# Column-quarter w_mod sums, host-made layouts, two-bank accounting and smaller first loads in a two-block transformer kernel

## The chip, the core and the metric

The program runs on one core of one Trainium2 chip. The metric is the device time of one execution in microseconds (us), taken as the median of three executions.

## What is computed

The reference takes 256 rows of 2048 features through two blocks, all in float32, batch 1.

Block one: `x + 0.5 * swiglu(rms_norm(x))` with inner width 5632; a mixer (`rms_norm(x) @ w_in`, grouped attention with rotary positions beside differential attention, `@ w_out`, residual); a second such feed-forward; a closing `rms_norm`.

Block two: two layers over x and, in layer 0, over a second stream, the context (256 rows of 2048). Each layer first makes modulation vectors, `silu(c) @ w_mod + b_mod` and `silu(c_ctx) @ w_mod + b_mod` (2048 x 6144 weights, one input row each), split into shift, scale and gate. The streams are normalised, scaled and shifted (`h = rms_norm(x) * (1 + scale) + shift`), projected by `w_in` (2048 x 6656), taken through pooling, neighbourhood attention (local window plus context keys, 16 heads of 64) and a depthwise convolution, gated, and projected by `w_out`. A last `rms_norm` closes it.

## The kernel before, in words

Every large product runs on TensorE (PE). Weights come in pieces of 512 x 512 (1 MB, `raw0` to `raw2`, three buffers), are split in halves of 256 rows by ScalarE (ACT) into `hi` (rounded to fp32r) and by VectorE (DVE) into `lo` (the rest), four halves in flight. Activations, transposed, lie in SBUF as operands `g` in the same two parts. For each contraction tile of 128 and each of two row tiles PE does three fp32r matmuls of 512 columns (`xh*hi`, `xh*lo`, `xl*hi`), so a piece is 24 matmuls and a half 12.

The program is written out instruction by instruction (`tc.manual_schedule`). `Net.run` walks the list of weight halves and emits their matmuls; after each group of three, `pump` lets "lanes" (Python generators: attention items, transposes, norms, convolution) emit their next steps. A planner keeps estimated clocks for PE, DVE and ACT (`tP`, `tD`, `tA`) and estimated end times of the last write (`W`) and read (`R`) of each tile. A lane that yields "pe" is resumed when `tP` has passed the lane's time `me.t` by 200 ns; after a load it waits 8000 ns (`DMA_LAT`, L32). So PE's order is fixed when the program is made, and where an estimate is early PE stands still on the chip.

PSUM: four banks belong to two jobs in turn, three are "side" banks for the lanes, one (`pv`) is for attention outputs. `get` (L312) hands out slots of a pool; for side banks it sets `me.t` to the time at which the last reader of the first slot handed out is done (L325). Attention items of block two (`item_x`, `item_c`) take two side banks at once, put the scores of one head of 64 in each, and read each by a maximum and an exponential.

At the start `consts` loads the identity and the gains of the first norm, `warm` (L715) issues WARM = 4 matmuls on zeros, and `first_loads` (L792) loads x by 512 columns between the first pieces. `next_norm` and `gain_op` transpose x on PE (four 128 x 128 per side bank, L252) and write the operand `f1h`. `setup_lane` (L727) starts at 25 us: silu of c, the other gains, the convolution taps and the lambda of block one; gains and taps are loaded as rows and transposed on PE.

`wmod_step` multiplies w_mod pieces of 128 x 1024 by the entries of the two input rows and adds them on DVE, so that a job (12 in all, 6 for each layer) ends with two accumulators of 128 x 1024, whose sums over the 128 partitions are wanted. `wmod_sum` (L919) splits each in hi and lo and multiplies it with a column of ones (`sel`): per accumulator two groups of 512 columns, in each a pair of fp32r matmuls, one row read out, one store.

`mod_op` (L1377) prepares the operand of a layer: load rows, scale by the row's 1/rms, transpose on PE, scale and shift, split. For the context of layer 0 it is `c0h`.

SP issues nearly all loads and stores, in program order. `mm`, `act`, `tt`, `stt` record each operation, so matmuls stand at L224, transposes at L252, ACT at L157, DVE at L167 and L176.

Of the kernel before, what the change touches and what calls it, by code (L numbers as in the profile page):

```python
# [16 lines left out]
D = 2048  # L17
# [14 lines left out]
DMA_LAT = 8000.0  # L32
WARM = 4
SLACK = [2500.0, 2000.0, 1500.0, 0.0, 0.0]
# [73 lines left out]
class Net:  # L108
# [338 lines left out]
    def run(self, seq):  # L447
# [14 lines left out]
        def fetch():  # L462
            while at["fetch"] < len(pieces):
# [23 lines left out]
                self.dmaT = max(self.dmaT, self.R.get(n, 0.0), self.tP - 8000) + t  # L487
                self.W[n] = max(self.dmaT, self.R.get(n, 0.0) + t + 2000)
# [57 lines left out]
        for h, (job, i, s) in enumerate(main):  # L546
# [22 lines left out]
            for z, kt in enumerate(kts):  # L569
# [5 lines left out]
                for t in range(2):  # L575
                    self.slot += 1
                    m = slice(t * 128, t * 128 + 128)
                    self.mm(job.ps[t], xh[:, m], hi[:, z, :], st, False, ready)
                    self.mm(job.ps[t], xh[:, m], lo[:, z, :], False, False, ready)
                    self.mm(job.ps[t], xl[:, m], hi[:, z, :], False, sp, ready)  # L580
# [100 lines left out]
    def consts(self):  # L681
# [11 lines left out]
        self.csil = self.cp.tile([128, 2, 16], F32, name="csil")  # L693
        self.sel = self.cp.tile([128, 2], F32R, name="sel")
        self.wleft = [6, 6]
# [5 lines left out]
        self.lam = self.keep(1)  # L701
        self.f1rows = self.cp.tile([16, 128], F32, name="f1rows")
# [3 lines left out]
    def consts_lane(self):  # L706
        b, = yield from self.get("side")
        ps = self.bank(b)
        self.tr(ps[:, :16], self.f1rows, self.ident[:16, :16])
        self.copy(self.fv[:, 0:16], ps[:, :16])  # L710
        self.rel(b)
        self.flags.add("f1gain")
        yield

# [12 lines left out]
    def setup_lane(self):  # L727
        a = self.a

        yield from self.after(25)  # L730
        s, s2 = yield from self.get("T2", 2)
# [3 lines left out]
        self.dma(c[:, 1, :], a["c_ctx_2"].rearrange("(p k) -> p k", p=128))  # L735
        self.dma(self.blob[:, 128:576], a["k_blob"][:, 128:576])
        yield "dma"
# [3 lines left out]
        self.ts(self.csil, c, 0.5)  # L741
        one = self.sb(s2, [128, 2])
        self.nc.vector.memset(one, 1.0)
        self.copy(self.sel, one)
        self.rel(s, s2)
        self.flags.add("cs")

        s, = yield from self.get("T2")
        fr = self.sb(s, [128, 128])
        for nm, key in (("mix_norm", "mix"), ("ffn2_norm", "f2"), ("norm_g_2", "ng0"), ("conv_dw_b_2", "cdb"),  # L750
                        ("conv_ln_g_2", "lng"), ("conv_ln_b_2", "lnb"), ("b_subln", "bsub"), ("pool_scale_2", "psc")):
            src = a[nm].rearrange("o (r c) -> (o r) c", c=128)
            self.dma(fr[FV[key] - 16:FV[key] - 16 + src.shape[0], :], src)
        yield "dma"
        b, = yield from self.get("side")
        ps = self.bank(b)
        n = NFV - 16
        self.tr(ps[:, :n], fr[:n, :], self.ident[:n, :n])
        yield "evA"
        self.copy(self.fv[:, 16:NFV], ps[:, :n])  # L760
        self.rel(b, s)
        yield "D"
# [3 lines left out]
        s, = yield from self.get("T2")  # L766
        w = self.sb(s, [128, 512])
        self.dma(w[:62, :], a["conv_dw_2"].rearrange("l k c -> (l k) c"))
        yield "dma"
        b, = yield from self.get("side")  # L770
        ps = self.bank(b)
        for i in range(4):
            self.tr(ps[:, i * 62:i * 62 + 62], w[:62, i * 128:i * 128 + 128], self.ident[:62, :62])
        yield "ev"
        self.copy(self.cdw.rearrange("p c k -> p (c k)"), ps[:, :248])
        self.rel(b, s)

# [14 lines left out]
    def first_loads(self, n):  # L792

        cs = slice(n * 512, n * 512 + 512)
        self.nc.sync.dma_start(out=self.x[:, :, cs], in_=self.xin[:, :, cs])
        self.dmaT += 1475
        for t in range(2):
            self.W[self.key(self.x[:, t, cs])] = self.dmaT

        def later(n=n, t=self.dmaT):  # L800
            yield from self.until("f1gain")
            while self.tP < t:
                yield lambda: self.tP >= t
            yield from self.next_norm("f1", n)

        self.spawn(later(), 0)

# [111 lines left out]
    def wmod_sum(self, job):  # L919

        l, c = job.wmod
        for r in range(2):
            hs, ls = yield from self.get("T4", 2)
            hi, lo = self.sb(hs, [128, 1024], F32R), self.sb(ls, [128, 1024], F32R)
            yield from self.lsplit(hi, lo, job.acc[r])
            self.rel(job.slots[r])
            for z in range(2):
                cs = slice(z * 512, z * 512 + 512)
                b, = yield from self.get("side")
                yield "pe"  # L930
                ps = self.bank(b)
                self.mm(ps[:2, :], self.sel, hi[:, cs], True, False)
                self.mm(ps[:2, :], self.sel, lo[:, cs], False, True)
                s, = yield from self.get("T2")
                yield "evA"
                row = self.sb(s, [128, 512])
                self.copy(row[:1, :], ps[:1, :])
                self.rel(b)
                yield "st"
                self.dma(self.modrows[l][r:r + 1, c * 1024 + z * 512:c * 1024 + z * 512 + 512], row[:1, :])  # L940
                self.rel(s)
            self.rel(hs, ls)
# [371 lines left out]
    def next_norm(self, f, n):  # L1314
# [3 lines left out]
        yield from self.gain_op(f + "h", n, self.x, f)  # L1318
        if f == "f1":
            self.cur.prio = 3  # L1320
            yield from self.after(22)
        for t in range(2):
            yield from self.sq_part(self.x[:, t, cs], ssp[:, 4 * t + n:4 * t + n + 1])
        self.vals[f + "_left"] -= 1
        if self.vals[f + "_left"] == 0:
# [51 lines left out]
    def mod_op(self, op, src, rstd, rflag, l, w):  # L1377
# [3 lines left out]
        for n in range(4):  # L1381
# [7 lines left out]
            for j in range(2):  # L1389
# [13 lines left out]
                yield  # L1403
            self.rel(*sl)

    def chunk_pieces(self, wt, col):
# [619 lines left out]
    def body(self, upto):  # L2026
# [9 lines left out]
        self.xin = a["x"][0].rearrange("(t p) d -> p t d", p=128)  # L2036
        self.dmaT = 3550.0
        self.vals = {}
# [23 lines left out]
        self.warm()  # L2062
        self.spawn(self.consts_lane(), 0)
        self.first_loads(0)
# [38 lines left out]


# [15 lines left out]
```

## Time and profile before

| What | Value |
|---|---|
| Median of 3 executions | 3276.68 us (3273.68 to 3277.45) |
| Profiled execution, its own time | 3275.49 us |
| Its span in the profile | 3273.7 us |
| PE busy | 3250.8 us, 99% |
| DVE busy | 2560.0 us, 78% |
| ACT busy | 1588.7 us, 49% |
| HBM read | 702.58 MB |

The page lists engines, the chain of work that ended last, and groups of instructions. A matmul on float32 tiles shows as two records, one on fp32r as one. "Busy" of PE counts a modelled end, so for prices the starts of the next instructions are used, not the durations. A wait is written "engine tile line <- what ended it".

### The profile page before, as it was taken

The page shows a single profiled execution, that of the slowest core. Times are in us where ns is not written, and L with a number is a line of the kernel's source. Part 1 is how long each engine was busy: PE and PEld are TensorE (multiplying, and loading weights), DVE is VectorE, ACT ScalarE, POOL GpSimd, SP SyncE. Part 2 cuts the span into 40 slices and gives each one's busy share as a digit, 9 for nine tenths or more (in the row PEclk, how much of TensorE's full clock was granted, in tenths as well). Part 3 has the DMA queues.
Part 4 walks back from the last instruction along what each step waited for, and adds up shares of the span by engine and source line. Part 5 has one row for each costly group of instructions (what it writes and reads, how often), then busy time and mean ns, then how long its engine had stood idle before and what let it go on. Part 6 is the DMA issues. An engine that isn't in the chain of part 4 may idle for free.

```text
span 3273.7 us, 40054 instructions
## 1 busy us (share of the span) xinstructions
PE 3250.8 (99%) x15284; PEld 2649.1 (81%) x15284; DVE 2560.0 (78%) x3418; ACT 1588.7 (49%) x2086; POOL 1.2 (0%) x11
## 2 busy tenths in 40 slices
PE   9999999999999999999999999999999999999998
PEld 7888888888888888888888877788877788887777
DVE  5998999866876689988888588666887676598766
ACT  5544444445555444444445554544454455445543
POOL 0000000000000000000000000000000000000000
PEclk9999999999999999999999999999999999999999
DMA  7877777755445677777776665477555576564555
GB/s 246 293 275 274 268 272 278 279 196 183 146 163 168 229 261 273 264 269 263 271 266 228 206 196 167 154 231 238 181 159 151 163 242 229 182 191 136 166 174 188
DMA packets 362581, 713.79 MB, mean 218 GB/s; under 512 B 40180, under 2 KB 43814, under 8 KB 362388
## 3 DMA queue, kind: packets, MB, share of 16 engines
q1 hardware_dynamic: 362388, 711.23, 65.2%
q8 instruction: 120, 1.97, 0.2%
q14 instruction: 73, 0.60, 0.0%
HBM read 702.58 MB, written 8.59 MB: 217 GB/s over the span
## 4 chain that ended last, share of the span: by engine, by line
PE 93%; DVE 3%; DMA 2%; issue 1%; ACT 0%; SPq 0%; ACTq 0%; DVEq 0%
PE mm L224 85%; PE side L252 4%; PE side L224 3%; DVE T L176 2%; DMA T<-in_na_rpb 1%; PE pv L224 1%; DVE lo L167 1%; DVE T L167 0%; DMA xs<-res 0%; ACT hi L157 0%; ACT T L157 0%; DMA res<-in_x 0%; SPq L258 0%; DVE sm L184 0%; DVE side L167 0%
## 5 line engine op out<-in xcount | busy, mean ns | idle before, releaser
L224 PE MATMUL mm<-hi,g 128*128 128x512 f32 x8576 | 2747.1, 394 | 0.7 <-ACT hi L157 0.7
L224 PEld LDWEIGHTS mm<-hi,g 128*128 128x128 f32 x8576 | 1612.6, 188 | 351.3 <-issue 17.9
L167 DVE TENSOR_TENSOR lo<-raw,hi 128x1024 fp32r<-128x1024 f32 (+1 forms) x1079 | 1312.1, 1221 | 480.1 <-ACT hi L157 477.6
L224 PE MATMUL mm<-lo,g 128*128 128x512 f32 x4288 | 1672.5, 390 | 0.4 <-DVE lo L167 0.4
L157 ACT ACTIVATE hi<-raw 128x1024 fp32r<-128x1024 f32 (+1 forms) x1079 | 1140.0, 1059 | 1096.0 <-PE mm L224 967.5
L224 PEld LDWEIGHTS mm<-lo,g 128*128 128x128 f32 x4288 | 807.4, 188 | 159.9 <-DVE lo L167 1.3
L176 DVE SCALAR_TENSOR_TENSOR T<-T,csil,T 128x1024 f32<-128x1024 f32 x360 | 445.2, 1278 | 0.0
L157 ACT ACTIVATE T<-side 128x512 f32<-128x512 f32 (+2 forms) x180 | 104.6, 584 | 183.2 <-PE side L252 130.4
L252 PEld LDWEIGHTS side<-blob,T 128*128 128x128 f32 (+1 forms) x1027 | 125.5, 140 | 37.3 <-issue 6.3
L252 PE MATMUL side<-blob,T 128*128 128x128 f32 (+1 forms) x1027 | 154.5, 274 | 0.1
L176 DVE SCALAR_TENSOR_TENSOR T<-Y,cdw,T 128x256 f32<-128x256 f32 x360 | 151.0, 478 | 0.0
L157 ACT ACTIVATE T<-side,sm 128x256 f32<-128x256 f32 (+1 forms) x131 | 74.9, 577 | 65.5 <-DVE sm L184 49.7
L157 ACT ACTIVATE T<-T 128x512 f32<-128x512 f32 (+5 forms) x91 | 65.6, 721 | 59.4 <-DVE T L167 47.2
L167 DVE TENSOR_TENSOR T<-T,T 128x512 f32<-128x512 f32 (+4 forms) x130 | 81.9, 651 | 7.3 <-ACT T L157 5.1
L224 PE MATMUL side<-T,T 128*128 128x256 f32 (+2 forms) x352 | 76.3, 377 | 7.6 <-ACT T L157 4.1
L184 DVE TENSOR_REDUCE sm<-side 128x1 f32<-128x512 f32 (+1 forms) x96 | 65.8, 690 | 11.3 <-PE side L224 8.8
L224 PEld LDWEIGHTS side<-T,T 128*128 128x128 f32 (+1 forms) x352 | 51.0, 188 | 25.8 <-issue 10.0
L157 ACT ACTIVATE g<-side 128x512 fp32r<-128x512 f32 (+1 forms) x58 | 32.9, 569 | 79.0 <-PE side L252 72.6
L176 DVE SCALAR_TENSOR_TENSOR res<-mm,res 128x512 f32<-128x512 f32 x96 | 61.6, 681 | 0.6 <-PE mm L224 0.6
L167 DVE TENSOR_TENSOR T<-T,blob 128x256 f32<-128x256 f32 (+2 forms) x80 | 39.4, 526 | 17.3 <-DMA T<-in_na_rpb 15.3
L157 ACT ACTIVATE T<-mm 128x512 f32<-128x512 f32 x66 | 38.7, 597 | 29.0 <-PE mm L224 25.6
L157 ACT ACTIVATE T<-mm,kp 128x512 f32<-128x512 f32 (+1 forms) x58 | 39.1, 682 | 26.3 <-PE mm L224 24.0
(99 smaller groups left out, 926.1 us busy)
## 6 DMA issues: line engine op xcount, KB each, us to landing
raw<-in_w_in SPq DMA_DIRECT2D x208, 1024.0 KB
raw<-in_ffn_w_gu SPq DMA_DIRECT2D x175, 1024.0 KB
T<-in_w_mod SPq DMA_DIRECT2D x192, 512.0 KB
raw<-in_ffn_w_down SPq DMA_DIRECT2D x88, 1024.0 KB
raw<-in_w_out SPq DMA_DIRECT2D x64, 1024.0 KB
T<-xs SPq DMA_DIRECT2D x32, 256.0 KB
T<-in_ctx SPq DMA_DIRECT2D x24, 256.0 KB
T<-in_na_rpb SPq DMA_DIRECT2D x64, 96.0 KB
```

Source lines behind the costliest of these rows:

```text
L157: self.nc.scalar.activation(out, in_, func, **kw)
L167: self.nc.vector.tensor_tensor(out=out, in0=in0, in1=in1, op=op)
L176: self.nc.vector.scalar_tensor_tensor(out=out, in0=in0, scalar=s, in1=in1, op0=op0, op1=op1)
L184: self.nc.vector.reduce_max(out=out, in_=in_, axis=AX.X, negate=True)
L224: self.nc.tensor.matmul(out, lhsT, rhs, start=start, stop=stop)
L252: self.nc.tensor.transpose(out, in_, self.ident if ident is None else ident)
```

## The change

Six things are done:

1. `wmod_sum` no longer splits. It multiplies the four accumulator halves as float32 with 32 columns of ones, each into 32 partitions of one side bank (column quarters 0, 32, 64, 96), reads the bank once and stores four rows.
2. `host_layouts` adds four inputs: x transposed in blocks, the context transposed, the gains as columns, the taps as columns. Block one's first operand comes from the transposed x (`first_op`), with no PE transposes. The rows of x are loaded later, with pieces 3 to 6, for the sums of squares (`first_sums`) and the residual. `setup_lane` starts at 45 us and has no transposes.
3. `ctx_op` takes the place of `mod_op` for `c0h`: it spreads the rows' 1/rms over all partitions by two float32 matmuls of ones with a diagonal, and multiplies the transposed context by it.
4. `get` sets `me.t` to the latest of all side banks handed out.
5. Loads at the start: x first, by half a block; piece 0 in three parts; the gains on ACT's queue; WARM = 6; the planner's first due times are altered.
6. In the first half the order is `xh*hi`, `xl*hi`, `xh*lo`.

```diff
-WARM = 4
+WARM = 6
...
         if pool == "side":
-            me.t = max(me.t, self.R.get(self.last.get(got[0]), 0.0))
+            me.t = max([me.t] + [self.R.get(self.last.get(g), 0.0) for g in got])
...
                 if p == 0:
-                    for z in range(2):
-                        self.nc.sync.dma_start(out=raws[p][:, 2 * z:2 * z + 2], in_=ap[:, 2 * z:2 * z + 2])
+                    for z in (slice(0, 1), slice(1, 2), slice(2, 4)):
+                        self.nc.sync.dma_start(out=raws[p][:, z], in_=ap[:, z])
...
-                if p < 3:
+                if p < 9:
                     self.first_loads(p + 1)
...
+                    three = [(xh, hi), (xh, lo), (xl, hi)]
+                    if h == 0:
+                        three = [three[0], three[2], three[1]]
...
-        nc.sync.dma_start(out=self.ident, in_=a["k_blob"][:, 0:128])
-        nc.sync.dma_start(out=self.f1rows, in_=a["ffn1_norm"].rearrange("o (r c) -> (o r) c", c=128))
+        nc.scalar.dma_start(out=self.fv, in_=a["h_fv"])
...
-        yield from self.after(25)
+        yield from self.after(45)
...
     def first_loads(self, n):
+        if n < 4:
+            if n == 0:
+                self.xT = [self.sb(self.pools["T4"].free.pop(0), [128, 4, 256]) for _ in range(4)]
+            for i, z in ((0, slice(0, 2)),) if n == 0 else ((0, slice(2, 4)), (1, slice(0, 4))) if n == 1 else ((n, slice(0, 4)),):
+                self.nc.sync.dma_start(out=self.xT[i][:, z], in_=self.a["h_x"][i][:, z])
+            gen = self.first_op
+        elif n < 8:
+            cs = slice((n - 4) * 512, (n - 4) * 512 + 512)
+            self.nc.sync.dma_start(out=self.x[:, :, cs], in_=self.xin[:, :, cs])
+            gen = self.first_sums
...
+    def first_op(self, n):
+        for zs in ((0,), (1,), (2, 3)) if n == 0 else ((0, 1), (2, 3)):
+            g = yield from self.gran("f1h", (4 * n) // 8)
+            part = [(4 * n + z, self.xT[n][:, z, :], self.fv[:, FV["f1"] + 4 * n + z:FV["f1"] + 4 * n + z + 1]) for z in zs]
+            for kt, src, f in part:
+                self.act(g[:, 0, kt % 8, :], src, AF.Copy, scale=f)
+            yield "D"
+            for kt, src, f in part:
+                self.stt(g[:, 1, kt % 8, :], src, f, g[:, 0, kt % 8, :].bitcast(F32), ALU.mult, ALU.subtract)
...
     def wmod_sum(self, job):
-        for r in range(2):
-            hs, ls = yield from self.get("T4", 2)
-            yield from self.lsplit(hi, lo, job.acc[r])
-            for z in range(2):
-                self.mm(ps[:2, :], self.sel, hi[:, cs], True, False)
-                self.mm(ps[:2, :], self.sel, lo[:, cs], False, True)
-                self.copy(row[:1, :], ps[:1, :])
+        for r in range(2):
+            for z in range(2):
+                q = 2 * r + z
+                self.mm(ps[32 * q:32 * q + 32, :], self.sel, job.acc[r][:, z * 512:z * 512 + 512], True, True)
+        self.copy(rows, ps)
+        for q in range(4):
+            self.dma(self.modrows[l][q // 2:q // 2 + 1, at:at + 512], rows[32 * q:32 * q + 1, :])
...
+    def ctx_op(self, op):
+        for t in range(2):
+            self.ts(dg[:, t, :], self.ident, rstd[:, t:t + 1])
+        for t in range(2):
+            self.mm(ps[:, t * 128:t * 128 + 128], self.ones, dg[:, t, :], True, True)
+        for z in range(2):
+            self.copy(R[:, z, :], ps[:, :256])
+        for n in range(4):
+            for j in range(2):
+                self.dma(v[j], self.a["h_ctx"][kt * 128:kt * 128 + 256].rearrange("(k p) t -> p k t", p=128))
+            for j in range(2):
+                self.tt(y, y, R, ALU.mult)
+                for z in range(2):
+                    self.affine(y[:, z, :], y[:, z, :], self.modA[0][:, 16 + kt + z:17 + kt + z], ...)
+                yield from self.lsplit(g[:, 0, k:k + 2, :], g[:, 1, k:k + 2, :], y)
...
-            self.spawn(self.mod_op("c0h", a["ctx_2"][0], self.vals["c0_rstd"], "c0_rstd", 0, 1), 1)
+            self.spawn(self.ctx_op("c0h"), 1)
...
+def host_layouts(a):
+    fv = np.concatenate([a[n].reshape(-1, 128).T for n in (
+    cdw = a["conv_dw_2"].reshape(62, 4, 128).transpose(2, 1, 0)
+    x = a["x"][0].T.reshape(4, 4, 128, T).transpose(0, 2, 1, 3)
+    return [("h_x", x), ("h_ctx", a["ctx_2"][0].T), ("h_fv", fv), ("h_cdw", cdw)]
```

## Rows read from the trace of the kernel before

**Rows 1.** The page's first part: busy us, share of the span, instructions.
```profile
PE 3250.8 (99%) x15284; PEld 2649.1 (81%) x15284; DVE 2560.0 (78%) x3418; ACT 1588.7 (49%) x2086; POOL 1.2 (0%) x11
```

**Rows 2.** The chain that ended last, in order of time: start us, us, what.
```profile
17.22 0.44 PE side L252 x4
...
1803.40 82.30 PE mm L224 x363
...
3168.99 0.86 PE side L224 x4
```

**Rows 3.** The waits of PE: what it waited for, total us, times, longest us.
```profile
PE side L224 <- ACT T L157: 5.1, 4, 2.6
PE side L224 <- DVE T L176: 3.5, 2, 1.8
```

**Rows 4.** One stretch, PE on tile mm alone: length, busy (instructions), clock, DMA, GB/s.
```profile
0.00:60.00 60.00, 48.79 (x197) 1.00 0.75 255
```

**Rows 5.** The timeline's first lines of PE: start us, us, engine, line, operation.
```profile
1.09 3.78 PE L224 MATMUL pv<-Y 128*128 128x256 f32 x8 [1.09 <-POOL Y L718]
...
9.08 0.80 PE L224 MATMUL mm<-hi,g 128*128 128x512 f32 x1 [0.66 <-ACT hi L157]
```

**Rows 6.** The chain's first load.
```profile
1.65 4.76 DMA res<-in_x
```

**Rows 7.** Stretches at the start: engines' busy (instructions), granted clock, DMA share, GB/s.
```profile
0.00:5.00 5.00, 3.91 (x9) 2.70 (x9) 0.00 (x0) 1.28 (x1) 0.51 (x5) 1.00 0.46 114
5.00:10.00 5.00, 2.86 (x10) 1.86 (x9) 1.46 (x4) 2.51 (x7) 0.23 (x2) 1.00 1.00 365
10.00:15.00 5.00, 4.93 (x17) 4.00 (x18) 3.31 (x7) 2.87 (x5) 0.00 (x0) 1.00 1.05 391
```

**Rows 8.** The page's groups of weight splits: busy us, mean ns, idle before.
```profile
L167 DVE TENSOR_TENSOR lo<-raw,hi 128x1024 fp32r<-128x1024 f32 (+1 forms) x1079 | 1312.1, 1221 | 480.1 <-ACT hi L157 477.6
...
L157 ACT ACTIVATE hi<-raw 128x1024 fp32r<-128x1024 f32 (+1 forms) x1079 | 1140.0, 1059 | 1096.0 <-PE mm L224 967.5
```

**Rows 9.** PE's timeline around one pair of w_mod's sums.
```profile
280.44 0.39 PE L224 MATMUL mm<-hi,g 128*128 128x512 f32 x1
280.66 0.63 PE L224 MATMUL side<-T,sel 128*2 128x512 f32 x2
...
281.36 0.39 PE L224 MATMUL mm<-lo,g 128*128 128x512 f32 x1
```

**Rows 10.** PE's timeline around one group on column halves.
```profile
2408.05 0.40 PE L224 MATMUL mm<-hi,g 128*128 128x512 f32 x1
2408.38 0.66 PE L224 MATMUL pv<-T,T 128*64 128x128 f32 x8
...
2409.75 0.40 PE L224 MATMUL mm<-lo,g 128*128 128x512 f32 x1
```

**Rows 11.** PE's timeline at two of the waits, in brackets the idle time.
```profile
2464.86 0.79 PE L224 MATMUL side<-T,T 64*128 64x256 f32 x1 [2.60 <-ACT T L157]
...
3015.79 0.48 PE L224 MATMUL side<-T,T 64*128 64x256 f32 x1 [1.31 <-ACT T L157]
```

**Rows 12.** Three stretches behind such waits; columns as in rows 7.
```profile
2395.57:2398.98 3.41, 3.41 (x12) 2.40 (x11) 2.04 (x5) 0.61 (x2) 0.00 (x0) 0.50 0.90 290
2463.84:2470.67 6.83, 5.82 (x15) 4.21 (x16) 6.50 (x12) 4.14 (x9) 0.00 (x0) 0.50 0.00 1
3016.80:3020.21 3.41, 3.41 (x9) 2.69 (x9) 3.31 (x8) 2.39 (x5) 0.00 (x0) 0.50 0.00 0
```

**Rows 13.** Loads of the attention bias in the chain.
```profile
2450.45 10.18 DMA T<-in_na_rpb
...
3002.67 8.89 DMA T<-in_na_rpb
```

**Rows 14.** The timeline from attention's last operand to the first output projection.
```profile
3156.79 0.69 DVE L176 SCALAR_TENSOR_TENSOR g<-T,g 128x512 fp32r<-128x512 f32 x1 [0.70 <-ACT g L157]
...
3174.69 0.40 PE L224 MATMUL mm<-hi,g 128*128 128x512 f32 x1
```

More of the change, by code (lines that the diff above doesn't have):

```diff
@@ L577, in run @@
                     m = slice(t * 128, t * 128 + 128)
-                    self.mm(job.ps[t], xh[:, m], hi[:, z, :], st, False, ready)
-                    self.mm(job.ps[t], xh[:, m], lo[:, z, :], False, False, ready)
-                    self.mm(job.ps[t], xl[:, m], hi[:, z, :], False, sp, ready)
+                    three = [(xh, hi), (xh, lo), (xl, hi)]
+                    if h == 0:
+                        three = [three[0], three[2], three[1]]
+                    for i, (xp, wp) in enumerate(three):
+                        self.mm(job.ps[t], xp[:, m], wp[:, z, :], st and i == 0, sp and i == 2, ready)
                     if z == 0 and t == 0:
@@ L701, in consts @@
         self.lam = self.keep(1)
-        self.f1rows = self.cp.tile([16, 128], F32, name="f1rows")
-        nc.sync.dma_start(out=self.ident, in_=a["k_blob"][:, 0:128])
-        nc.sync.dma_start(out=self.f1rows, in_=a["ffn1_norm"].rearrange("o (r c) -> (o r) c", c=128))
[L706 to L713, printed above, removed]
+        nc.scalar.dma_start(out=self.fv, in_=a["h_fv"])
+        self.act(self.small(1), self.ones[:, :1], AF.Copy)
     def warm(self):
@@ L741, in setup_lane @@
         self.ts(self.csil, c, 0.5)
-        one = self.sb(s2, [128, 2])
-        self.nc.vector.memset(one, 1.0)
-        self.copy(self.sel, one)
+        self.nc.vector.memset(self.sel, 1.0)
         self.rel(s, s2)
         self.flags.add("cs")
[L748 to L762, printed above, removed]
         self.ts(self.fv[:, FV["bsub"]:FV["bsub"] + 2], self.fv[:, FV["bsub"]:FV["bsub"] + 2], self.sub_scale)
         self.flags.add("fv")
[L766 to L776, printed above, removed]
         s, = yield from self.get("T2")
@@ L792, in first_loads @@
     def first_loads(self, n):
[L794 to L801, printed above, removed]
+        if n < 4:
+            if n == 0:
+                self.xT = [self.sb(self.pools["T4"].free.pop(0), [128, 4, 256]) for _ in range(4)]
+                self.xTslots = [f"T4_{i}" for i in range(4)]
+            for i, z in ((0, slice(0, 2)),) if n == 0 else ((0, slice(2, 4)), (1, slice(0, 4))) if n == 1 else ((n, slice(0, 4)),):
+                self.nc.sync.dma_start(out=self.xT[i][:, z], in_=self.a["h_x"][i][:, z])
+            self.dmaT += (737, 2212, 1475, 1475)[n]
+            self.W[self.key(self.xT[n])] = self.dmaT
+            gen = self.first_op
+        elif n < 8:
+            cs = slice((n - 4) * 512, (n - 4) * 512 + 512)
+            self.nc.sync.dma_start(out=self.x[:, :, cs], in_=self.xin[:, :, cs])
+            self.dmaT += 1475
+            for t in range(2):
+                self.W[self.key(self.x[:, t, cs])] = self.dmaT
+            gen = self.first_sums
+        else:
+            return
@@ L802, in later @@
+        def later(n=n % 4, t=self.dmaT):
             while self.tP < t:
                 yield lambda: self.tP >= t
-            yield from self.next_norm("f1", n)
-        self.spawn(later(), 0)
+            yield from gen(n)
+        self.spawn(later(), 0 if n < 4 else 3)
+    def first_op(self, n):
[7 more added lines that the diff above has]
+                self.stt(g[:, 1, kt % 8, :], src, f, g[:, 0, kt % 8, :].bitcast(F32), ALU.mult, ALU.subtract)
+                self.setop("f1h", kt, g, kt % 8)
+            yield
+        self.rel(self.xTslots[n])
@@ L921, in wmod_sum @@
         l, c = job.wmod
+        b, = yield from self.get("side")
+        yield "pe"
+        ps = self.bank(b)
         for r in range(2):
[L923 to L926 removed]
             for z in range(2):
[L928 to L931, printed above, removed]
[L932 to L942 removed]
+                q = 2 * r + z
+                self.mm(ps[32 * q:32 * q + 32, :], self.sel, job.acc[r][:, z * 512:z * 512 + 512], True, True)
+        self.rel(*job.slots)
+        s, = yield from self.get("T2")
+        yield "evA"
+        rows = self.sb(s, [128, 512])
+        self.copy(rows, ps)
+        self.rel(b)
+        yield "st"
+        for q in range(4):
+            at = c * 1024 + q % 2 * 512
+            self.dma(self.modrows[l][q // 2:q // 2 + 1, at:at + 512], rows[32 * q:32 * q + 1, :])
+        self.rel(s)
         self.wleft[l] -= 1
@@ L1404, in mod_op @@
             self.rel(*sl)
+    def ctx_op(self, op):
+        rstd = self.vals["c0_rstd"]
+        yield from self.until("c0_rstd", "mod0")
+        yield from self.gran(op, 0)
+        sr, = yield from self.get("T2")
+        R = self.sb(sr, [128, 2, 256])
+        b, = yield from self.get("side")
+        s, = yield from self.get("T2")
+        dg = self.sb(s, [128, 2, 128])
+        for t in range(2):
+            self.ts(dg[:, t, :], self.ident, rstd[:, t:t + 1])
+        yield "pe"
+        ps = self.bank(b)
+        for t in range(2):
+            self.mm(ps[:, t * 128:t * 128 + 128], self.ones, dg[:, t, :], True, True)
+        yield "evA"
+        for z in range(2):
+            self.copy(R[:, z, :], ps[:, :256])
+        self.rel(b, s)
+        for n in range(4):
+            sl = yield from self.get("T2", 2)
+            v = [self.sb(x, [128, 2, 256]) for x in sl]
+            for j in range(2):
+                kt = 4 * n + 2 * j
+                self.dma(v[j], self.a["h_ctx"][kt * 128:kt * 128 + 256].rearrange("(k p) t -> p k t", p=128))
+            yield "dma"
+            for j in range(2):
+                kt = 4 * n + 2 * j
+                y = v[j]
+                self.tt(y, y, R, ALU.mult)
+                g = yield from self.gran(op, kt // 8)
+                for z in range(2):
+                    self.affine(y[:, z, :], y[:, z, :], self.modA[0][:, 16 + kt + z:17 + kt + z],
+                                self.modT[0][:, 48 + kt + z:49 + kt + z])
+                k = kt % 8
+                yield "A"
+                yield from self.lsplit(g[:, 0, k:k + 2, :], g[:, 1, k:k + 2, :], y)
+                self.setop(op, kt, g, k)
+                self.setop(op, kt + 1, g, k + 1)
+                yield
+            self.rel(*sl)
+        self.rel(sr)
     def chunk_pieces(self, wt, col):
@@ L2110 @@
     arrays, args = {}, {}
-    for name, v in [(n, inputs[n]) for n in _INS] + list(host_consts().items()):
+    for name, v in [(n, inputs[n]) for n in _INS] + list(host_consts().items()) + host_layouts(inputs):
         v = np.ascontiguousarray(v)
```

26 lines of the change are left out of this document (18 added, 8 removed).

## The prediction

> **What bounds the kernel now.** Begin with the engines: PE is busy for 99% of the span, DVE for 78%, ACT for 49% [rows 1]. So what matters is PE's own work and the few places where it stands still; work taken from DVE or ACT is worth nothing by itself. Next, the chain of waits gives PE's prices: 363 weight matmuls in a row take 82.30 us, 0.2267 each, so a piece of 24 costs 5.44 us; a group of four transposes costs 0.44; four records of 256 columns, which are two float32 matmuls, cost 0.86, so float32 costs 1.68 ns per column and a 512-column matmul, alone, 0.86 [rows 2]. Next, PE's waits: after the start nearly all idle time is in six waits of score matmuls in side banks, 8.6 us together [rows 3]. Last, the start: by 60 us PE has done 197 weight matmuls, worth 44.7 us, so 15.3 us went elsewhere [rows 4]. Durations come from the profiled execution (3275.49 us, 1.2 below the median of 3276.68); I sum against it and add 1.2 at the end. A difference of 0.2%, 6.6 us, is about what a measurement of this kernel can tell from none.
>
> **The start.** Of those 15.3 us, eight groups of transposes of x are 3.5 and the transposes of gains and taps under 1; the rest is a late and halting begin: the first weight matmul starts at 9.08 us [rows 5], after 512 KB of x that were issued at 1.65 and landed 4.76 later [rows 6]. The change issues x at about 0.7, behind nothing, and half as much. It takes 0.9 off for the issue and 0.9 for 256 KB at some 280 GB/s, so x is there near 4.6. One scaling on ACT, about 0.5, and a quarter piece of weights a microsecond behind x make a first matmul possible near 6.3. The four warm-up matmuls took 3.78 [rows 5]; six take 5.7 and end at 6.8, so they set it: about 6.8 instead of 9.08.
>
> Data then sets the pace. Piece 1 is ready when 3.0 MB have come (half a MB of x and one of weights for each of two pieces). The trace moved 0.57 MB by 5 us and 2.4 by 10, then 391 GB/s [rows 7]. By that, less 0.7 us for the two constant loads that no longer stand ahead, 3.0 MB have moved at 10.8. The x of before had moved by 5 us and was signalled at 6.41, so 1.4 more: 12.2. Then a split on ACT (1.06) and on DVE (1.22) [rows 8]: 14.5. The `lo` product is second in its piece, so piece 1 begins at 14.3, and PE's stream is as if begun at 14.3 - 5.44 = 8.9 us. That replaces 15.3: **6.4 us gained**. Ends: if only transposes go, 3.5; if supply keeps up with the first matmul at 6.8, 8.5.
>
> The rows of x, 2 MB, now come beside pieces 3 to 6: 1.5 MB per 5.44 us is 276 GB/s, under the 391 seen, with three raw buffers as cover; without that cover 2 MB cost 5.4 us. The sums of squares come later; they gate the reading of job 0's banks, which job 2 needs only after eight pieces (43.5 us). On SP a dozen small loads of the set-up leave, four of x enter ahead of weights already two pieces early, and the gains go to ACT's queue, idle then. The set-up's delay from 25 to 45 us ends near 54 us (its load plus 8), just as the first w_mod piece is fetched. The new product order in the first half lets two products run before `lo`; it is inside the 8.9.
>
> **w_mod's sums.** Twelve jobs with two accumulators of two halves make 48 pairs of `sel` matmuls. Around one pair PE's steps run from 280.44 to 281.36; less two steps of 0.2267 the pair costs 0.47 [rows 9], all of them 22.4 us. Now each of 12 jobs has four float32 matmuls of 512 columns on column quarters. Quarters do not occur before; halves do. An attention output group has eight float32 matmuls of 128 columns on two halves: one after another they would take 8 x 128 x 1.68 = 1.72, yet the group costs 2409.75 - 2408.05 - 0.45 = 1.25 [rows 10]. Two halves thus run beside each other: 0.86, and 0.39 for going in and out. Four quarters beside each other would cost 0.86 + 0.39 = 1.25 a job; two at a time 2.11; one after another 3.83. The low end is 0.86, entry hidden. I take 1.25, since the halves lose nothing to each other: 15.0 us, **7.4 gained**. The ends are 12.1 gained and 23.6 lost.
>
> The Trainium skill ("TensorE: Matmul & The Clock Gate", "Part 3: Packing small matmuls") has three column tiles of 32 at 512 columns giving 2.38 times, not 3. By that share four would take about 1.09 instead of 0.86, an estimate, and the gain would be 4.6 instead of 7.4; no row here shows more than two.
>
> The splits that leave (24 on each of ACT and DVE) and three of four bank reads were hidden by PE and count nothing; nor do four stores per job, as before, now together on SP.
>
> **Context operand.** Eight groups of transposes go (eight times 0.44); two float32 matmuls of 128 columns come, 0.43 with entry: **3.1 gained**. DVE gets a full multiply instead of the faster scaling, a few us while f2's last jobs cover it; uncovered it would be under 3 us.
>
> **Two banks.** The six waits [rows 3] all stand in groups that took two banks: the first bank's matmuls run, then PE waits for a reader of the second, 2.60 us at the longest [rows 3, 11]. Single-bank groups by the hundred show none. That is what the accounting of the first slot alone would do. Moreover three stretches right behind such waits were granted 0.50, which is 1.2 GHz, 13.65 us in all [rows 12]; PE had stood still just before each fall, for 1.3 us in the shortest case and 2.6 in the longest [rows 11]. Of these 12.6 are busy, half of it lost: 6.3. At stake: 8.6 + 0.6 (my estimate for restarting the array) + 6.3 = 15.5. With the latest bank counted the item is emitted later and PE does weight matmuls meanwhile; nothing else is queued behind the wait, as it is in the lane.
>
> Not all need go. The waits at 2461 and 3014 (2.6 and 1.3, with 6.8 and 3.4 us of half clock) follow bias loads that took 10.18 and 8.89 us where the planner counts 8 [rows 13], so its time for the second bank is early too. They hold 3.9 + 4.6 = 8.5; I take 5.2 of them, and all 7.0 of the others: **12.2 gained**, with ends 0 and 15.5.
>
> **Sum.** 6.4 + 7.4 + 3.1 + 12.2 = 29.1. 3275.5 - 29.1 = 3246.4, plus 1.2: **3247.6 us**.
>
> **Rivals.**
> *Banks not helped.* The second reader is late on the chip, not in the book. The late loads [rows 13] speak for it in two cases; before the other waits I see none. Then 12.2 stays: 3259.8.
> *Quarters in part or not side by side.* Four moving streams might share what two do not need to. Two at a time: 10.3 worse, 3257.9. One after another: 31.0 worse, **3278.6**, no change. The halves [rows 10] speak against it.
> *Slower: attention becomes the bound.* Items now hold back until both of two banks, out of three, are read. Each layer over x has 16 items; their results gate the output projection. In the last layer the last operand is written at 3157.5, and the first output matmul starts at 3174.7: 17.2 us to spare [rows 14]. If every item lost the longest wait, 2.6, 16 x 2.6 - 17.2 = 24.4 us per layer would show, 48.8 in two: 3296.4. It decides the sign from 2.2 us per item on. Against it: an item could not finish its scores earlier before, when PE itself stood waiting.
>
> **How the numbers follow.** Forecast 0.68, its own range 3238 (start 8.5, quarters 12.1, banks 15.5) to 3256 (start 3.5, banks 7). Banks not helped 0.12; two quarters at a time 0.04; one after another 0.11; attention as bound 0.05. Faster by over 0.2% are the first three: 0.84. One after another lies at no change, 0.08 of its 0.11 within 0.2%, the rest slower: with attention 0.08. The range 3238 to 3263 leaves out these two and a fringe of the others, in all just under 0.2.
>
> **What would show it.** Start: first weight matmul near 6.8 and some 225 of them by 60 us. Sums: 12 groups of 1.25 us with their four quarters starting within tens of ns; steps of 0.86 mean one after another. Context: no transposes of it on PE. Banks: PE's waits on side banks under 3 us, at most one stretch of half clock before the end. Wrong would be a first operand projection of a layer, or an output projection, that waits for its operand, or weight matmuls that wait for `raw` in the first 60 us.

## The result and the profile after

The changed kernel takes 3241.90 us (median of four, 3240.93 to 3242.59), the kernel before 3275.48 beside it: a ratio of 0.9897, 95% interval 0.988 to 0.9914, 33.6 us less. Predicted were 3247.6 with 3238 to 3263 around it. The sign, the forecast case and the range held; the gain is 33.6 where the sum had 29.1. The profiled execution has a span of 3240.5.

Read it in the order of the prediction. The page's first part answers [rows 1]: every engine has a little less to do, and PE is still busy for 99% of a shorter span.

```profile
PE 3223.1 (99%) x15222; PEld 2630.0 (81%) x15222; DVE 2529.4 (78%) x3390; ACT 1550.0 (48%) x2031; POOL 1.3 (0%) x12
```

Next the waits of PE (total us, times, longest), beside [rows 3]: the six waits in side banks, 8.6 us, have become two of 0.98 and 0.84. What is left besides stands at the start, one wait each for ACT, POOL and DVE, but for one of 0.3 in the middle.

```profile
PE mm L224 <- ACT hi L157: 2.1, 1, 2.1
PE side L224 <- DVE T L176: 1.8, 2, 1.0
PE pv L224 <- POOL Y L714: 1.2, 1, 1.2
PE mm L224 <- DVE lo L167: 0.8, 1, 0.8
```

Then single stretches, columns as in [rows 4, 7]: first PE on tile `mm` alone, then all engines at the start, then two around the attention stretches that [rows 12] had at half clock.

```profile
0.00:60.00 60.00, 51.03 (x213) 0.97 0.85 297
```

```profile
10.00:15.00 5.00, 3.31 (x8) 2.42 (x9) 4.13 (x8) 4.44 (x8) 0.00 (x0) 0.71 1.04 399
12.13:15.54 3.41, 3.35 (x8) 2.67 (x9) 3.01 (x7) 2.85 (x5) 0.00 (x0) 0.50 1.04 393
2370.00:2480.00 110.00, 109.02 (x629) 85.34 (x628) 91.40 (x165) 58.32 (x91) 0.23 (x2) 1.00 0.55 155
2990.00:3020.00 30.00, 30.00 (x172) 23.70 (x171) 23.63 (x42) 14.77 (x23) 0.00 (x0) 1.00 0.45 143
```

In the middle of the kernel the granted clock is now 1.00 throughout: every stretch of 30 us from 30 to 3210 reads so. At the start it is not: 3.41 us at 0.50, which is 1.2 GHz, from 12.13 on. For the kernel before the column reads 1.00 there [rows 4, 7], but its records go at half pace too: from 10.66 to 11.94 its weight matmuls start 0.43 us apart, as in the stretch at 0.50 here, and not 0.23.

```profile
10.66 1.05 PE L224 MATMUL mm<-hi,g 128*128 128x512 f32 x2
11.51 0.63 PE L224 MATMUL mm<-lo,g 128*128 128x512 f32 x1
```

So in the first microseconds of a span the pace has to be read from the records and not from the column. By 60 us PE has done 213 weight matmuls instead of 197 [rows 4]; 225 were predicted.

Lines of the timeline of PE and ACT (start, us, engine, line, operation, idle before it) and the chain of waits, both of the start, show why. They answer to [rows 5, 6].

```profile
1.24 4.85 PE L224 MATMUL pv<-Y 128*128 128x256 f32 x12 [1.24 <-POOL Y L714]
5.74 0.81 PE L224 MATMUL mm<-hi,g 128*128 128x512 f32 x2
9.02 0.91 ACT L157 ACTIVATE g<-T,fv 128x256 fp32r<-128x256 f32 x2 [2.62 <-DMA T<-in_h_x]
10.93 0.50 PE L224 MATMUL mm<-hi,g 128*128 128x512 f32 x1 [2.09 <-ACT hi L157]
12.19 0.79 PE L224 MATMUL mm<-lo,g 128*128 128x512 f32 x1 [0.76 <-DVE lo L167]
```

```profile
2.59 6.41 DMA T<-in_h_x
...
9.02 0.91 ACT g L157 x2
9.93 0.96 ACT hi L157
...
10.91 1.24 DVE lo L167
...
12.19 43.84 PE mm L224 x185
56.03 0.44 PE side L252 x4
...
58.55 0.44 PE side L252 x4
```

The first product starts at 5.74, a microsecond before the forecast; of the twelve warm-up records the third to the tenth each start 0.43 us after the one before, the last two 0.25 and 0.22. But the second half of x's first block is issued behind all of piece 0's weights, 1 MB, and lands at 9.00. ACT has its scaling next, stands 2.62 us for it, and the weight split of piece 0's second half is queued behind. PE waits 2.09 us for that split, then 0.76 for the `lo` part, and the stretch at half clock follows. From 12.19 on it never waits again for weights.

PE's timeline around one job of `wmod_sum` answers to [rows 9]:

```profile
172.78 0.39 PE L224 MATMUL mm<-hi,g 128*128 128x512 f32 x1
173.10 1.06 PE L224 MATMUL side<-T,sel 128*32 128x512 f32 x8
...
174.43 0.39 PE L224 MATMUL mm<-lo,g 128*128 128x512 f32 x1
```

From 172.78 to 174.43 are 1.65 us; less two steps of 0.2267 this job costs 1.20, where 1.25 were taken; the twelve cost 1.20 to 1.31, 14.9 in all. The first records of the four quarters start at 173.098, .105, .111 and .118: all four run at once.

The tiles `sel` and `ones`, grouped over the whole kernel (the three numbers are the shortest, median and longest in ns):

```profile
L224 PE MATMUL side<-T,sel x96: 592/605/617, 173.1 to 1734.7; 128*32 128x512 f32 x96
```

```profile
L224 PE MATMUL side<-T,ones x4: 272/275/275, 1730.5 to 1730.9; 128*128 128x128 f32 x4
```

That is twelve jobs of eight records, and two float32 matmuls for the context.

Last, in the chain, the two late bias loads, an undisturbed group of scores and the end, beside [rows 13, 14]:

```profile
2359.68 10.00 DMA T<-in_na_rpb
...
2902.80 9.99 DMA T<-in_na_rpb
...
3109.33 1.06 PE side L224 x8
...
3155.09 68.73 PE mm L224 x303
```

Two bias loads, the first of each layer, still take 10.00 and 9.99 us and stand before the two waits of 0.98 and 0.84. The last 303 weight matmuls, which hold the output projection, run in 68.73 us, 0.2268 each, with no wait: attention did not become the bound.

### The profile page after: what moved, and what is told of

Read it like the earlier page. It is cut to its first block, busy times and chain, and to the rows that moved or that the text cites. A ratio compares the mean times of both kernels' runs of the same rounds, so it can differ in the third digit from the quotient of the medians.

```text
span 3240.5 us, 39759 instructions
## 1 busy us (share of the span) xinstructions
PE 3223.1 (99%) x15222; PEld 2630.0 (81%) x15222; DVE 2529.4 (78%) x3390; ACT 1550.0 (48%) x2031; POOL 1.3 (0%) x12
## 4 chain that ended last, share of the span: by engine, by line
PE 96%; DVE 2%; DMA 1%; issue 1%; ACT 0%; SPq 0%; ACTq 0%; DVEq 0%
PE mm L224 88%; PE side L252 4%; PE side L224 3%; PE pv L224 1%; DVE T L176 1%; DMA T<-in_na_rpb 1%; DVE lo L167 1%; DVE T L167 0%; DMA T<-in_h_x 0%; ACT hi L157 0%; ACT T L157 0%; DVE mm L167 0%; SPq L258 0%; SPq L480 0%; DVE sm L176 0%
## 5 line engine op out<-in xcount | busy, mean ns | idle before, releaser
L157 ACT ACTIVATE T<-side 128x512 f32<-128x512 f32 (+1 forms) x149 | 85.9, 581 | 140.8 <-PE side L252 99.8
L252 PEld LDWEIGHTS side<-blob,T 128*128 128x128 f32 x990 | 121.1, 140 | 34.4 <-issue 3.6
L252 PE MATMUL side<-blob,T 128*128 128x128 f32 x990 | 148.2, 273 | 0.3 <-DVE T L172 0.3
L157 ACT ACTIVATE T<-T 128x512 f32<-128x512 f32 (+4 forms) x67 | 40.5, 604 | 59.0 <-DVE T L167 46.8
L167 DVE TENSOR_TENSOR T<-T,T 128x512 f32<-128x512 f32 (+3 forms) x114 | 58.2, 535 | 2.2
L157 ACT ACTIVATE T<-mm 128x512 f32<-128x512 f32 x72 | 42.0, 598 | 32.7 <-PE mm L224 29.2
L172 DVE TENSOR_SCALAR T<-T,sm 128x512 f32<-128x512 f32 (+1 forms) x120 | 48.6, 422 | 2.1
```

The costliest lines, as they stand in the source:

```text
L157: self.nc.scalar.activation(out, in_, func, **kw)
L167: self.nc.vector.tensor_tensor(out=out, in0=in0, in1=in1, op=op)
L172: self.nc.vector.tensor_scalar(out=out, in0=in0, scalar1=s1, scalar2=s2, op0=op0, **kw)
L252: self.nc.tensor.transpose(out, in_, self.ident if ident is None else ident)
```

## The experiments

The kernel before took 3277.2, 3277.7 and 3278.0 us beside the three sets of runs that follow, 3275.5 beside the changed kernel; that took 3241.9 and, again in the third set, 3242.3. Differences of a microsecond or two between sets are therefore not read; within the third set they are.

**One bank counted, in the changed kernel.**

```diff
-            me.t = max([me.t] + [self.R.get(self.last.get(g), 0.0) for g in got])
+            me.t = max(me.t, self.R.get(self.last.get(got[0]), 0.0))
```

> The changed kernel with the one line on side banks undone: `get` counts the first bank alone again. Theory (the two-bank accounting is the largest part of the 33.6 us): waits of score matmuls on side banks come back, 6 to 10 us of them in place of 1.8, with two or three stretches of half clock behind them, and the time is 3254 to 3260 us, 12 to 18 above the changed kernel's 3241.9. Rival (the waits of before were of that one program's order, and the other parts' new order would have moved them away in any case): no more than 3 us of such waits and 3241 to 3246 us.

Measured: 3259.51 (3258.65 to 3261.01), ratio 0.9948 [0.9934, 0.9963]: 17.6 us over the changed kernel. Its waits, two stretches behind them (columns as in [rows 7]), and two stalled groups in PE's timeline:

```profile
PE side L224 <- ACT T L157: 6.1, 4, 2.6
PE side L224 <- DVE T L176: 3.7, 2, 1.8
```

```profile
2381.11:2384.52 3.41, 3.41 (x10) 2.64 (x9) 3.27 (x6) 2.91 (x6) 0.00 (x0) 0.50 0.78 258
2449.37:2452.78 3.41, 3.41 (x10) 2.28 (x8) 3.31 (x8) 2.73 (x6) 0.00 (x0) 0.50 0.00 0
```

```profile
2445.50 0.70 PE L224 MATMUL side<-T,T 64*128 64x256 f32 x2
2448.78 0.48 PE L224 MATMUL side<-T,T 64*128 64x256 f32 x1 [2.59 <-ACT T L157]
2448.79 0.48 PE L224 MATMUL side<-res,T 64*128 64x256 f32 x1
2449.10 0.38 PE L224 MATMUL side<-T,T 64*128 64x256 f32 x1
2449.11 1.21 PE L224 MATMUL side<-res,T 64*128 64x256 f32 x3
2450.25 0.79 PE L224 MATMUL mm<-hi,g 128*128 128x512 f32 x1
...
2996.71 0.70 PE L224 MATMUL side<-T,T 64*128 64x256 f32 x2
2998.70 0.48 PE L224 MATMUL side<-T,T 64*128 64x256 f32 x1 [1.30 <-ACT T L157]
...
2999.76 0.50 PE L224 MATMUL mm<-hi,g 128*128 128x512 f32 x1
```

The waits are back, and behind two of the six the half clock too. The waits are 9.8 against 1.8, so 8.0; the two stretches lose half of 6.8, so 3.4. That leaves 6 us, and the groups of records show most of it. Undisturbed, the eight records of two heads cost 1.06 (the chain above), because the two heads, on 64 rows each, run side by side: the pairs at 2448.78 and 2448.79 and at 2449.10 and 2449.11 start 10 ns apart. The first stalled group takes 4.75, its wait is 2.59, so 1.10 is lost beside the wait: the first head's first two records ran alone before it, the second head's last two alone behind it, and the end of the group ran at half clock. The second stood at full clock and takes 3.05 with a wait of 1.30: 0.69 is lost because the heads run one behind the other. Six groups stall here and two in the changed kernel, so four times 0.69, 2.8 us.

The same loss occurs where the waits show next to nothing. By the order of the records PE there goes on with the first head while the second's bank is late, hardly stands, and has the heads out of step: five groups here take 0.3 to 0.7 us longer than undisturbed with no wait over 0.12, 2.5 in all, and one in the changed kernel 0.5. With these 2.0 the sum is 8.0 + 3.4 + 2.8 + 2.0 = 16.2; the two profiled spans differ by 16.4.

**Two banks counted, in the kernel before**: the same line, the other way round.

> The kernel before with that one line alone. Theory: idle time of PE on side banks falls from 8.6 us to under 3, the three stretches of half clock go or one stays, and the time is 3258 to 3263 us, 12 to 17 below 3275.5. Rival (late bias loads and not the book-keeping make the waits): 3268 to 3275 us with waits of 5 us or more.

Measured: 3257.09 (3256.67 to 3257.71), ratio 0.9941 [0.9926, 0.9955]: 20.1 us faster, more than expected. The waits in side banks, and the stretch that held 10.24 us of half clock [rows 12]:

```profile
PE side L224 <- DVE T L176: 1.4, 2, 0.9
```

```profile
2380.00:2480.00 100.00, 99.11 (x557) 77.14 (x555) 82.09 (x151) 53.16 (x84) 0.23 (x2) 1.00 0.55 152
```

One line, alone, takes all of this half clock away and 7.2 of the 8.6 us of waits, and needs nothing else of the change. The rival, that the second reader is late on the chip only, falls.

**w_mod's sums as before**, with their splits and pairs.

```diff
+        for r in range(2):
+            yield from self.lsplit(hi, lo, job.acc[r])
+            for z in range(2):
+                self.mm(ps[:2, :], self.sel, hi[:, cs], True, False)
+                self.mm(ps[:2, :], self.sel, lo[:, cs], False, True)
```

> The changed kernel with the old `wmod_sum`: splits on ACT and DVE, 48 pairs of fp32r matmuls. Theory (only PE's steps count): 48 x 0.47 = 22.6 us in place of 12 x 1.20 = 14.4, so 3249 to 3251 us, 7 to 9 above 3241.9. Rival (the splits that left, 24 x 1.05 on ACT and 24 x 1.22 on DVE, were worth something too): 3254 us or more, with new waits of PE for ACT or DVE between 170 and 1760 us.

Measured: 3250.40 (3249.45 to 3250.85), ratio 0.9920 [0.9903, 0.9936]: 8.5 us slower. PE's steps alone, 22.6 for the 48 pairs against 14.9 for the twelve jobs, give 7.7. One wait is new, and the profiled start had no stretch of half clock behind its first products, where the changed kernel's had one; the two work against each other. Whether the wait comes from the splits that are back or from the later end of the sums is not shown.

```profile
PE side L252 <- DVE T L167: 1.7, 1, 1.7
```

```profile
0.00:60.00 60.00, 51.48 (x218) 1.00 0.87 305
```

**All four sums in one quarter.**

```diff
-                self.mm(ps[32 * q:32 * q + 32, :], self.sel, job.acc[r][:, z * 512:z * 512 + 512], True, True)
+                self.mm(ps[0:32, :], self.sel, job.acc[r][:, z * 512:z * 512 + 512], True, True)
```

> The changed kernel with all four float32 matmuls of a w_mod job written to the same 32 partitions, so that one follows another; three of the four sums are lost and the fourth is stored in all four places. Theory (quarters run beside each other because they are different columns): a job costs 3.5 to 3.9 us in place of 1.20, 28 to 32 us more in all, 3270 to 3274 us. Rival (float32 of 32 columns is cheap wherever it lies): 3242 to 3245 us.

Measured: 3272.16 (3270.39 to 3275.82), ratio 0.9987 [0.9977, 0.9996]: 30.3 us slower. The same job in its timeline:

```profile
171.60 0.39 PE L224 MATMUL mm<-hi,g 128*128 128x512 f32 x1
171.92 3.62 PE L224 MATMUL side<-T,sel 128*32 128x512 f32 x8
...
175.81 0.40 PE L224 MATMUL mm<-lo,g 128*128 128x512 f32 x1
```

From 171.60 to 175.81, less 0.45, a job costs 3.75; the twelve cost 45.1 against 14.9, so 30.2. The same four matmuls with the same operands cost three times as much when they share 32 partitions. What makes the new sums cheap is the quarters; sharing the partitions also means writing the same addresses, and the run doesn't separate the two.

**The context operand by rows**: `mod_op` again.

```diff
-            self.spawn(self.ctx_op("c0h"), 1)
+            self.spawn(self.mod_op("c0h", a["ctx_2"][0], self.vals["c0_rstd"], "c0_rstd", 0, 1), 1)
```

> The changed kernel with the context operand of layer 0 made by the old `mod_op`, from rows with eight groups of transposes. Theory (each group of PE work is on the path at 0.44 us): 3.1 us more, 3244.5 to 3245.5 us. Rival (its place in the order has room, or the fuller multiply on DVE costs as much as the transposes): 3241 to 3243 us.

Measured: 3245.00 (3244.39 to 3245.27), ratio 0.9901 [0.9886, 0.9915]: 3.1 us slower, the predicted 3.1. By ratios alone the two kernels' intervals overlap; the runs themselves don't overlap with those of the changed kernel in either set, and the count of transposes gives the same size.

**x by rows**, transposed on PE in eight groups again.

```diff
-            gen = self.first_op
...
+            yield from self.gain_op("f1h", n, self.x, "f1")
```

> The changed kernel with block one's first operand made as before: x loaded by rows between the first pieces, eight groups of transposes on PE, identity loaded first; gains still as columns. Theory (the start's gain is the transposes and the earlier begin): what PE spends beside weight matmuls by 60 us goes from 11.7 back to 14 to 16 us, and the time is 3244 to 3246 us, 2 to 4 above 3241.9. Rival (the start is set by the arrival of weights either way): within 1 us of 3241.9.

Measured: 3244.61 (3244.38 to 3244.88), ratio 0.9900 [0.9883, 0.9916]: 2.7 us slower. The weight matmuls by 60 us:

```profile
0.00:60.00 60.00, 48.87 (x207) 1.00 0.76 258
```

That is 207 against 213, though eight groups of 0.44 would be 15 matmuls: this kernel had no stretch of half clock behind its first products, which gave part of it back. Against the 218 of the kernel with the old sums, which had none either, it is 11.

**WARM = 4**, the two more warm-up matmuls left out.

> The changed kernel with four warm-up matmuls in place of six. Theory (the two more only fill PE's time until the first weights are split, at 5.7 us, and keep it busy): the first weight matmul does not start earlier, some of the first ones go at half the pace, and the time is 0 to 2 us above 3241.9. Rival (six hold the first weight matmul back): 0.3 to 1 us below 3241.9.

Measured: 3241.84 (3241.40 to 3244.63), ratio 0.9893 [0.9878, 0.9908]: no difference. The rival's 0.3 to 1 us are not there, and the theory's first point, that the first product doesn't start earlier, is wrong. PE's timeline has the first product 0.44 us earlier, and the next products halting for ACT and DVE (0.29 and 0.22 us); then PE waits at the same point as the changed kernel for the same split:

```profile
5.30 0.73 PE L224 MATMUL mm<-hi,g 128*128 128x512 f32 x2 [0.28 <-ACT hi L157]
...
10.94 0.49 PE L224 MATMUL mm<-hi,g 128*128 128x512 f32 x1 [1.28 <-ACT hi L157]
```

So the warm-up does set the first product, as the prediction had it, and the first product sets nothing: PE goes on at 10.94 here and at 10.93 there.

**Finer first loads.** The chain above says which load is late, so: x's second half goes between the quarters of piece 0's weights, the next block's second half between the halves of piece 1, and piece 0's second half is split by contraction tile and multiplied in the new order too.

```diff
-                    for z in (slice(0, 1), slice(1, 2), slice(2, 4)):
-                        self.nc.sync.dma_start(out=raws[p][:, z], in_=ap[:, z])
+                    for z in (0, 1, None, 2, 3):
+                        if z is None:
+                            self.nc.sync.dma_start(out=self.xT[0][:, 2:4], in_=self.a["h_x"][0][:, 2:4])
...
-                for z in range(2) if h == 0 else [slice(0, 2)]:
+                for z in range(2) if h < 2 else [slice(0, 2)]:
```

> The changed kernel with finer first loads: the second half of the first x block before the last half of piece 0, that half in two parts, piece 1 in two halves with x between them, and the first two halves of weights split by contraction tile. Theory (PE's 2.5 us and 1.3 us of steps at 8.5 and 10.9 us are a load order: ACT stands for x behind 512 KB of weights, and the split behind it): the stream begins some 2 to 3.5 us earlier, 3238 to 3240 us. Rival (bytes, not order, set the begin: by 9 us 1.5 MB are in, and 3 MB by 13): 3241 to 3242.5 us, with the same idle time a little later.

Measured: 3240.80 (3239.43 to 3241.80), ratio 0.9888 [0.9873, 0.9903]: 1.1 us, between the theories. The wait of 2.1 at 8.8 us is gone; another of 1.25 stands at 12 us, and 0.8 on `lo` remains. In this execution a stretch of half clock followed again (15.27 to 18.69), with 215 matmuls by 60 us. The same kernel was therefore run again, beside the changed one and one step further: piece 1's first half in two loads, four halves taken by contraction tile, and the second half of block 1's scaling on ACT held back behind the split that PE waits for (the edit is against the finer loads).

```diff
-                for z in range(2) if h < 2 else [slice(0, 2)]:
+                for z in range(2) if h < 4 else [slice(0, 2)]:
...
+            if n == 1 and zs == (0, 1):
+                t1 = self.tP + 2700
+                while self.tP < t1:
+                    yield lambda: self.tP >= t1
```

> The changed kernel as it is, as the measure for the two beside it on the same chip: 3241 to 3243 us.

> The finer first loads once more, on the same chip as the changed kernel. Theory (the idle time moved from 8.8 to 12 us and shrank from 2.9 to 2.0): 0.5 to 1.5 us below the changed kernel. Rival (nothing was gained, 1.1 us was scatter): within 0.4 us of it.

> The finer first loads, with the first half of piece 1 in two parts, four halves of weights split by contraction tile, and the operands of the sixth and seventh contraction tile held back by 2.7 us of the planner's time, so that ACT does not stand for them ahead of the weights. Theory (the wait at 12 us is again order: ACT queues a split behind an operand that is needed 2.7 us later): no wait of PE over 0.6 us between 5.6 and 30 us, no half clock after 10 us, 3238 to 3240 us. Rival (bytes set the begin): the wait moves on to the next half and the time stays within 0.7 us of the kernel with finer loads.

Measured: 3242.25 (3241.58 to 3243.20) for the changed kernel, 3240.19 (3238.95 to 3241.23) for the finer loads, and 3239.34 (3238.64 to 3239.68) one step further: ratios 0.9891 [0.9874, 0.9907], 0.9885 [0.987, 0.9899] and 0.9882 [0.9867, 0.9897]. The last kernel's longest wait at the start, and its start; both stretches stand beside those of the changed kernel above.

```profile
12.53 0.73 PE L224 MATMUL mm<-hi,g 128*128 128x512 f32 x2 [0.44 <-ACT hi L157]
```

```profile
0.00:60.00 60.00, 53.40 (x226) 1.00 0.86 309
```

```profile
10.00:15.00 5.00, 4.56 (x20) 3.13 (x19) 4.05 (x9) 3.95 (x9) 0.00 (x0) 1.00 1.05 401
```

It moves as much between 10 and 15 us as the changed kernel, 401 against 399 GB/s, and does 20 matmul records instead of 8. Order set the start more than bytes: which transfer stands ahead of which on SP, and which scaling ahead of which split on ACT. (By 10 us the last kernel had moved 2.74 MB and the changed one 2.57, some 0.4 us of loading.) Part of the difference is the half clock, which the last kernel did not have here. Its 2.9 us lie under 0.2% and are seen by the runs not overlapping in one set. It is the fastest version of this study.

## Why the prediction came out as it did

**The start: a mis-sized term.** Predicted 6.4, measured about 4.5. By 60 us 213 weight matmuls are worth 48.3, so 11.7 went elsewhere; 0.9 of that are two groups of transposes at 56 and 58.6 us that belong to later work. So 10.8 replace 15.3. Counted by the 231st weight matmul, near 64 us, the changed kernel is 4.47 ahead. The step that failed is "PE's stream is as if begun at 14.3 - 5.44 = 8.9 us": I asked when piece 1 had been moved, forgot the order within piece 0, and counted the new start at full pace. The second half of x's block is behind 512 KB of weights that are not wanted before it, and its scaling ahead of a weight split on ACT. Piece 1 (the 25th weight matmul) began at 16.4, not 14.3. The half clock from 12.13 to 15.54, some 1.7 us, was not in the sum, and neither was that the 15.3 of before held some 1.6 us of half pace. The kernels with the old sums and with one quarter have the changed kernel's start and had no half clock after 10 us: 218 matmuls by 60 us, which by the same reckoning gains 5.6. So of the 1.9 that are missing, about 1.1 is the clock and the rest the order. That the warm-up sets the first product was right, 0.6 to 1.1 us too late (6.17 in the changed kernel's second profile); that it matters is what fell. The last kernel, with 226 matmuls by 60 us, shows that the forecast's 225 were there to be had.

**w_mod's sums: right.** 1.25 a job was forecast from the halves in [rows 10], 1.20 to 1.31 measured, 14.9 for the twelve; with 22.4 for the pairs of before that is 7.5 gained by the steps against 7.4 forecast. Undone, it costs 8.5, with the wait that is new there. Four quarters cost little more than the 0.86 that one such matmul was reckoned at, and 3.75 in one quarter. What I left open, whether four streams share something that two do not, is settled for this shape. The rivals of two at a time and one after another fall. The Trainium skill ("TensorE: Matmul & The Clock Gate", "Part 3: Packing small matmuls") has 2.38 times for three column tiles, from which the estimate was 1.09 + 0.39 = 1.48 a job; 1.20 to 1.31 was measured here, so the measurement decides, for four quarters of float32 and 512 columns.

**Context: right**, 3.1 by the count. The multiply on DVE showed in no wait.

**Two banks: right in mechanism, too small in size.** Predicted 12.2 with 15.5 as the most; undone it costs 17.6, alone it gives 20.1. Two steps failed. First, "At stake: 8.6 + 0.6 (my estimate for restarting the array) + 6.3 = 15.5": no run shows the 0.6. In its place the heads that no longer run side by side cost 0.69 in each stalled group, and 0.3 to 0.7 in groups without a wait to see. In the kernel before with two banks counted, 7.2 us of waits, 6.3 of half clock, 2.8 in four stalled groups and 1.9 in the others go: 18.2, where the profiles from the first attention on differ by 18.5. Second, I held back 3.3 us for two late bias loads. With the later bank counted, no wait for them is left: in the changed kernel DVE waits 7.9 us for bias loads in all instead of 15.3, and not at all for the two at these places, issued at 2441.0 and 2984.1 and used 7.8 us later. The 10.18 and 8.89 us of before were thus not bound to these loads; why they took less in the new order is not shown. Each layer's first load is late as before, before waits of 0.98 and 0.84.

**Attention as the bound: fell.** No output projection waits, and the last stretch of 303 matmuls has no wait. The bound that the prediction gave for it was reckoned loosely: 2 x (16 x 2.0 - 17.2) already uses up 29.1, so the sign turns at 2.0 us per item, and 2.2 is where it would be slower by 0.2%.

**The sum.** 4.5 + 7.5 + 3.1 + 17.6 = 32.7, against 33.6 measured. Read along the kernel, by the start of the same weight matmul in both profiles, the changed kernel is 4.5 ahead at 64 us, 16.1 at 1913 and 33.7 at the end: 4.5 for the start, 11.6 for sums and context, 17.6 for attention. Part of the forecast's nearness is luck: the start came 1.9 short and the banks gave 5.4 more than their terms, and the two errors have opposite signs. The agreement of the measured terms is also better than they deserve: the start varies by a microsecond between executions, and the effect of the two banks is 17.6 or 20.1 by the side it is taken from (16.4 and 18.5 by the profiles, from 1913 us on). Not tried singly: the planner's altered first due times, the gains on ACT's queue, the new product order and the gains' and taps' lost transposes.

## What to carry to other kernels

When a planner fixes the order of an engine's work, a group that takes several buffers must be timed by the latest of them: a wait inside such a group costs the wait, the concurrency of the group's parts, and sometimes (here behind two or three of six) the clock behind it. At a start, don't ask when the bytes are there, but walk each queue in order, SP's and ACT's, and ask what stands ahead of the item that the bound engine wants next. Reductions over partitions with one useful row each can share a bank by column quarters at little more than the price of one.

## What the hardware showed that was not expected

The clock at the start differed between executions of the same instructions. The changed kernel's first profile stood 2.09 and 0.76 us and then had 3.41 us at 0.50; its second stood 1.44 and 0.76 and had such a stretch a good microsecond later. The kernels with the old sums and with one quarter, whose start is the same program, stood 1.0 and 1.3 us, then 0.76, and had none (218 matmuls by 60 us against 213 and 212). The finer loads stood 1.2 and 0.8 us in both of their profiles; one had a stretch of 3.41 at 0.50, the other none:

```profile
0.00:60.00 60.00, 52.15 (x224) 1.00 0.87 309
```

It had 224 matmuls by 60 us against 215 in the first, 2.0 us, for the same program. In the middle it was the same: of the six waits in one bank counted, 1.3 to 2.6 us and one of 0.8, two were followed by half clock, and one of 1.83 was while another of 1.83 was not. So in these runs a wait of a microsecond or two was sometimes followed by half clock and sometimes not; what decides is not shown. A single profile of a start with such a wait can be off by 2 us, and the finer loads' first run by itself (1.1) may have understated the edit (2.1 in the third set).
